# A head's half-tile products in one row, their operands partly in places of the mix, and the first decay differences held on VectorE

## The chip, the core and the metric

The kernel runs on one core of a Trainium2 chip. The core has four compute engines that run their own queues side by side: TensorE (PE, matmuls), VectorE (DVE), ScalarE (ACT) and GpSimd (POOL). SyncE (SP) issues most of the DMAs. The metric is the time on the device in microseconds (us); the median of the runs is compared.

## The reference

The program is a trunk of two decoder layers over 256 tokens of width 2048. Layer 0 mixes by chunked gated linear attention (GLA) with 4 heads (key width 256, value width 384), layer 1 by forgetting attention (FoX) with 12 heads. Both also attend to 256 memory tokens with 4 heads, and both end in a gated MLP with a short convolution. What matters here is the part of GLA inside a chunk, where each product of query and key carries a decay of its own:

```python
bcum = jnp.cumsum(gc, axis=2)
rel = bcum[:, :, :, None, :] - bcum[:, :, None, :, :]
decay = jnp.exp(jnp.where(tri, rel, -jnp.inf))
att = jnp.einsum('bhtk,bhsk,bhtsk->bhts', qc, kc, decay)
o_intra = jnp.einsum('bhts,bhsv->bhtv', att, vc)
```

and in FoX the difference of the summed log forget gates that is added to each logit:

```python
s = s + ci[..., None] - c[:, :, None, :]
```

## The kernel before

**Projections.** Nearly all the time goes into projections with float32 weights. A unit of weights comes in by DMA (line 198), ScalarE rounds it to float32r ("whi", L201), and VectorE makes the rest ("wlo", L210, the weight split). TensorE then makes three products of the rounded parts. `proj_fm` (L235, L236, L238) gives features by tokens, with 512 moving columns for whi (both parts of the activations) and 256 for wlo. `proj_tm` (L272, L273, L274) gives tokens by features. Whi and wlo have three buffers each, so a late split stops TensorE at the next L236 or L273.

**GLA.** For each head, `gates` makes the running sums of the log gates (L550 on TensorE, L553 to L555 on ScalarE, L557 to L559 on VectorE). Projections give q ("gq"), k ("gk") and v ("gv"); the v of head 0 is made ahead of everything else. Head 3 has two output gates ("og") between k and v. `core` then makes the 256x256 matrix `att` of a head:

- Products over chunk borders: q1 and k1 carry the decay to a border (L569 to L581); L585 is a 128x128 product, L589 are 4 half-tile products (a 128x64 weight tile, which goes to one half of the array and of PSUM's partitions), and L595 are 8 half-tile products of plain k and q for the diagonal.
- Inside chunks, three levels (blocks of 64, 16 and 4 tokens). For each level VectorE makes decay differences in `dd` (three L614), ScalarE their exponentials (L615), VectorE the product with q (three L617); for two of the levels k is scaled as well (L623 to L625, into `ks`). Then come 8 half-tile products (L631), and 6 predicated copies per level (L643) put the results into `att` by a mask.

`dd` has one buffer and the PSUM places of the tag "s" are two, used by each of these groups, by the gate matmuls (L550) and elsewhere. At the end L650 and L651 multiply `att` with v, and L659 applies the norm.

**FoX.** `attend` fetches a head's row of summed gates from DRAM (L749) and makes the differences `dm` on VectorE (L751, L753). It multiplies q and k (L755, L756), takes the softmax (L763, L765) and multiplies with v (L772, L773).

**Order.** The kernel is written in a tile framework. It gives every engine a fixed order of instructions from the order of the code, from priorities (weight loads and splits stand 300 steps ahead, `AHEAD`) and from its own estimate of when data is ready. On the chip each engine works through its queue in that order, and waits on semaphores. `tc.issue_after(i)` keeps an instruction behind another one in this order.

`bufA` and `bufB` are 16 tiles of 128 x 2 x 256 each. In GLA bufB holds the layer's input and bufA takes the result (`mix`), tile by tile: 12 to 15 from the memory attention, 0 to 11 from the output gates in `take_og`. Before that, bufA holds the memory tokens.

Of the kernel before, what the change touches and what calls it, by code (L numbers as in the profile page):

```python
# [19 lines left out]
P = 128  # L20
# [118 lines left out]
def _trunk(ctx: ExitStack, tc: tile.TileContext, xt, xtok, memt, wp, wgu, gns, gfin, cnv, par, msk, out):  # L139
# [28 lines left out]
    bufA = [const.tile([P, 2, T], F32R, name=f"A{i}") for i in range(KC)]  # L168
# [11 lines left out]
    loads, casts = [], []  # L180
# [67 lines left out]
    def proj_tm(key, src, evac, spare=None):  # L248

        units = where[key]
        n = units[0][2]
        base = min(min(u[1]) for u in units)
        acc = [pacc.tile([P, 512], F32, name="acc", tag="acc") for _ in range(2)]
        ahead = 0 if spare is None else 4
        ready = {}
        for i in range(len(units) + ahead):
            for b, u in ((0, i), (1, i - ahead)):
                if not 0 <= u < len(units):  # L260
                    continue
                if b == 0:
                    ready[u] = split_unit(units[u], pool=wpool if spare is None or u < 3 else spare)
                hi, lo = ready[u]
                kcs = units[u][1]
                a = acc[b][:, :n]
                xs = slice(b * P, (b + 1) * P)
                for j, kc in enumerate(kcs):
                    s = slice(j * n, (j + 1) * n)
                    xk = src[kc - base]  # L270
                    last = u == len(units) - 1 and j == len(kcs) - 1
                    TE.matmul(a, xk[:, 0, xs], hi[:, s], start=u == 0 and j == 0, stop=False)  # L272
                    TE.matmul(a, xk[:, 0, xs], lo[:, s], start=False, stop=False)  # L273
                    TE.matmul(a, xk[:, 1, xs], hi[:, s], start=False, stop=last)  # L274
                if u == len(units) - 1:
                    evac(b, a)
# [226 lines left out]
    def gla(nx):  # L503
        h, mix = bufB, bufA
        with tc.tile_pool(name="gla", bufs=1) as gp:
            att = [gp.tile([P, 3 * P], F32, name=f"att{i}") for i in range(2)]
            ks = [gp.tile([P, 2, T], F32, name=f"ks{i}") for i in range(2)]
# [54 lines left out]
            def core(hd, q, k, v, bc):  # L562
# [3 lines left out]
                q1 = gp.tile([P, 2, T], F32, name="gq1", tag="gq1")  # L566
                k1 = gp.tile([P, 2, T], F32, name="gk1", tag="gk1")
# [18 lines left out]
                for c in range(2):  # L586
                    for b in range(2):
                        lhs = k1[:, c, 128:192] if b else k1[:, c, 192:]
                        TE.matmul(ps[64 * b : 64 * (b + 1), P : P + 64], lhs, q1[:, c, P * b : P * b + 64],  # L589
                                  start=c == 0, stop=c == 1)  # L590
                for b in range(2):
                    for c in range(2):
                        for g in range(2):
                            gs = slice(b * P + 64 * g, b * P + 64 * (g + 1))
                            TE.matmul(ps[64 * g : 64 * (g + 1), T + b * 64 : T + (b + 1) * 64], k[:, c, gs], q[:, c, gs],  # L595
                                      start=c == 0, stop=c == 1)
                a3 = at.rearrange("p (b t) -> p b t", t=P)[:, 0:3:2, :]
# [3 lines left out]
                for g in range(2):  # L601
                    gs = slice(64 * g, 64 * (g + 1))
                    og = a3[gs, :, gs]
                    V.copy_predicated(og, ident[gs, gs].bitcast(I32).unsqueeze(1).to_broadcast(og.shape),
                                      ps[gs, T : T + P].rearrange("p (b t) -> p b t", t=64))
                for li, B in enumerate(LEVELS):
                    H = B // 4
                    ps = work("s", 2)
                    dd = gp.tile([P, 8, NVER], F32, name="gdd", tag="gdd")
                    b4, q4 = (t.rearrange("p d (g n t) -> p (d g) n t", g=4, t=B) for t in (bc, q))  # L610
                    parts = [(dd[:, :, o : o + w].rearrange("p a (n t) -> p a n t", t=(3 - i) * H), (i + 1) * H)
                             for i, (o, w) in enumerate(VERSIONS)]
                    for d, t0 in parts:
                        V.tensor_tensor(d, b4[:, :, :, t0:], b4[:, :, :, t0 - 1 : t0].to_broadcast(d.shape), ALU.subtract)  # L614
                    S.activation(dd, dd, AF.Exp, scale=1.0 / TAU)  # L615
                    for d, t0 in parts:
                        V.tensor_tensor(d, d, q4[:, :, :, t0:], ALU.mult)  # L617
                    if H > 1:
                        kt = ks[li % 2]
                        de = gp.tile([P, 2, T], F32, name="gde", tag="ed", bufs=2)  # L620
                        b5, k5, e5, kt5 = (t.rearrange("p d (n r t) -> p (d n) r t", r=4, t=H)[:, :, :3, :]
                                           for t in (bc, k, de, kt))
                        V.tensor_tensor(e5, b5[:, :, :, H - 1 :].to_broadcast(e5.shape), b5, ALU.subtract)  # L623
                        S.activation(e5, e5, AF.Exp, scale=1.0 / TAU)
                        V.tensor_tensor(kt5, k5, e5, ALU.mult)  # L625
                    else:
                        kt = k
                    for b in range(2):
                        for c in range(2):
                            for g in range(2):  # L630
                                TE.matmul(ps[64 * g : 64 * (g + 1), b * NVER : (b + 1) * NVER],  # L631
                                          kt[:, c, b * P + 64 * g : b * P + 64 * (g + 1)],
                                          dd[:, 4 * c + 2 * b + g, :], start=c == 0, stop=c == 1)
                    p3 = ps[:, : 2 * NVER].rearrange("p (b c) -> p b c", b=2)
# [52 lines left out]
            for j in range(OG_EARLY, 6):  # L687
                take_og(j)


    def fox(nx, vt):
        hk, hq, mix = bufB, bufA, bufB
        stash = vt.rearrange("p b (i t) -> p (b i) t", t=T)
        with (
# [39 lines left out]
            def take_mq(j):  # L734
                def evac(c, a):
                    q = fp.tile([P, T], F32, name="mq", tag="tmp", bufs=5)
                    V.scalar_tensor_tensor(q, whole(a), -(HD ** -0.5), nx.row(), ALU.mult, ALU.mult)
                    mem_attention(fp, 1, q, 2 * j + c, mix)

                proj_fm(("mq", 1, j), hq, evac)  # L740

            for j in range(2):
# [4 lines left out]
            def attend(hd, q):  # L747
# [3 lines left out]
                V.scalar_tensor_tensor(dm[:, :P], pb[:, :P], cc[:, 0, hd : hd + 1], foxmask[:, P:],  # L751
                                       ALU.subtract, ALU.add)
                V.scalar_tensor_tensor(dm[:, P:], pb[:, :T], cc[:, 1, hd : hd + 1], foxmask, ALU.subtract, ALU.add)  # L753
# [231 lines left out]
```

## Time and profile before

| | |
|---|---|
| median of 3 runs | 2298.16 us (2298.02 to 2298.43) |
| the profiled execution | 2298.03 us, span 2296.2 us |
| granted TensorE clock | 0.999 |
| TensorE busy | 2284.1 us (99%) |
| VectorE busy | 1619.1 us (71%) |
| ScalarE busy | 1253.6 us (55%) |
| HBM traffic | 186 GB/s over the span |

The span runs from the first to the last instruction of the profile. A row of the timeline has the start in us from the span's start, the time of the merged instructions in us, the engine, the line, the operation, the tiles it writes and reads, the shape and the number of instructions; in brackets stands the idle time before it and what ended that. The ends of matmuls are modelled and overlap, so start times tell what TensorE takes. A float32 matmul that is not float32r leaves two records. A row of a group has the number of instructions, then the busy time, the mean of one in ns, and the idle time before.

### The profile page before, as it was taken

The numbers are of one execution on the slowest core, as the hardware profiler recorded it, in microseconds if no ns is written. First come the engines' busy times: TensorE is split into PE (matmuls) and PEld (weight loads), VectorE is DVE, ScalarE is ACT, GpSimd is POOL, SyncE is SP. The second block draws the span as 40 slices with busy tenths as digits, with TensorE's granted clock in tenths as the row PEclk, the third lists the DMA queues.
The fourth block names the chain that finished last, engine by engine and source line by source line (L and its number), as shares of the span: only waits on it lengthen the run. The fifth ranks groups of instructions, "written<-read, shape, count | busy, mean of one in ns | idle before, by whom it ended". The sixth has DMA issues, their size and how long they took to land.

```text
span 2296.2 us, 33165 instructions
## 1 busy us (share of the span) xinstructions
PE 2284.1 (99%) x12384; PEld 1976.2 (86%) x12384; DVE 1619.1 (71%) x2667; ACT 1253.6 (55%) x1967; POOL 3.1 (0%) x20
## 2 busy tenths in 40 slices
PE   9999999999999999999999999999999999999998
PEld 7889888888888888888888998888888888888886
DVE  7578987577765777557767557657776577756775
ACT  7555555555553555445565455556554455534554
POOL 0000000000000000000000000000000000000000
PEclk9999999999999999999999999999999999999999
DMA  8655455555555555555555664555555555665554
GB/s 320 196 162 161 156 164 179 187 184 189 190 189 194 188 191 187 193 192 191 186 183 187 182 194 152 170 193 184 188 189 192 192 191 186 191 193 192 185 192 156
DMA packets 124745, 430.15 MB, mean 187 GB/s; under 512 B 14108, under 2 KB 18600, under 8 KB 124456
## 3 DMA queue, kind: packets, MB, share of 16 engines
q1 hardware_dynamic: 124152, 427.24, 57.3%
q8 instruction: 97, 1.59, 0.3%
q10 hardware_dynamic: 432, 0.79, 0.1%
q14 instruction: 64, 0.52, 0.1%
HBM read 425.87 MB, written 2.11 MB: 186 GB/s over the span
## 4 chain that ended last, share of the span: by engine, by line
PE 99%; DMA 0%; DVE 0%; ACT 0%; issue 0%; DVEq 0%; ACTq 0%; SPq 0%
PE acc L235 37%; PE acc L236 20%; PE acc L273 12%; PE acc L274 12%; PE acc L272 12%; PE acc L238 2%; PE ps_s L842 0%; PE ps_s L631 0%; PE ps_t L402 0%; PE ps_s L409 0%; PE ps_o L420 0%; PE ps_s L756 0%; PE ps_o L772 0%; PE ps_o L650 0%; DMA raw<-wp 0%; DMA cb<-cdram 0%
## 5 line engine op out<-in xcount | busy, mean ns | idle before, releaser
L210 DVE TENSOR_TENSOR wlo<-raw,whi 128x1024 fp32r<-128x1024 f32 (+4 forms) x812 | 972.8, 1199 | 542.3 <-ACT whi L201 531.3
L201 ACT ACTIVATE whi<-raw 128x1024 fp32r<-128x1024 f32 (+4 forms) x812 | 843.5, 1040 | 778.4 <-PE acc L274 373.7
L235 PE MATMUL acc<-B,whi 128*128 128x512 f32 x1980 | 683.6, 395 | 0.0
L235 PE MATMUL acc<-A,whi 128*128 128x512 f32 x1680 | 580.9, 397 | 1.3 <-DVE A L310 1.3
L236 PE MATMUL acc<-B,wlo 128*128 128x256 f32 x2112 | 550.0, 281 | 0.0
L236 PE MATMUL acc<-A,wlo 128*128 128x256 f32 x1792 | 464.0, 281 | 0.0
L235 PEld LDWEIGHTS acc<-B,whi 128*128 128x128 f32 x1980 | 360.7, 188 | 68.5
L236 PEld LDWEIGHTS acc<-B,wlo 128*128 128x128 f32 x2112 | 397.4, 188 | 21.9
L235 PEld LDWEIGHTS acc<-A,whi 128*128 128x128 f32 x1680 | 305.7, 188 | 58.7 <-DVE A L310 2.0
L236 PEld LDWEIGHTS acc<-A,wlo 128*128 128x128 f32 x1792 | 338.3, 189 | 20.2
L273 PE MATMUL acc<-wlo,B 128*128 128x512 f32 (+3 forms) x736 | 274.8, 374 | 0.9 <-DVE wlo L210 0.9
L274 PE MATMUL acc<-whi,B 128*128 128x512 f32 (+3 forms) x736 | 273.6, 372 | 0.0
L272 PE MATMUL acc<-whi,B 128*128 128x512 f32 (+3 forms) x736 | 247.2, 372 | 0.0
L273 PE MATMUL acc<-wlo,A 128*128 128x512 f32 x544 | 212.3, 390 | 0.0
L274 PE MATMUL acc<-whi,A 128*128 128x512 f32 x544 | 211.8, 389 | 0.0
L272 PE MATMUL acc<-whi,A 128*128 128x512 f32 x544 | 192.4, 390 | 0.0
L243 ACT ACTIVATE part<-acc 128x256 f32<-128x256 f32 x240 | 89.9, 375 | 156.7 <-PE acc L238 156.6
L273 PEld LDWEIGHTS acc<-wlo,B 128*128 128x128 f32 x736 | 138.2, 188 | 20.5 <-DVE wlo L210 1.2
L274 PEld LDWEIGHTS acc<-whi,B 128*128 128x128 f32 x736 | 138.2, 188 | 18.6
L272 PEld LDWEIGHTS acc<-whi,B 128*128 128x128 f32 x736 | 137.3, 188 | 18.7
L245 DVE TENSOR_TENSOR wholes<-acc,part 128x256 f32<-128x256 f32 x240 | 101.2, 422 | 64.2 <-ACT part L243 63.9
L274 PEld LDWEIGHTS acc<-whi,A 128*128 128x128 f32 x544 | 102.2, 188 | 21.1
(213 smaller groups left out, 1578.5 us busy)
## 6 DMA issues: line engine op xcount, KB each, us to landing
raw<-wp SPq DMA_DIRECT2D x743, 512.0 KB, 3.4
raw<-wp SPq DMA_DIRECT2D x32, 384.0 KB, 3.1
raw<-wp SPq DMA_DIRECT2D x24, 388.0 KB, 3.1
raw<-wp SPq DMA_DIRECT2D x8, 400.0 KB, 3.1
xf<-xt SPq DMA_DIRECT2D x16, 128.0 KB, 4.4
x<-xtok SPq DMA_DIRECT2D x4, 512.0 KB, 7.5
mt<-memt SPq DMA_DIRECT2D x3, 512.0 KB, 6.8
cb<-cdram SPq DMA_DIRECT2D x12, 128.0 KB, 3.2
```

What stands on the lines that cost most here:

```text
L201: casts.append(S.activation(hi[:, s], raw[:, s], AF.Copy))
L210: V.tensor_tensor(lo[:, s], raw[:, s], hi[:, s].bitcast(F32), ALU.subtract)
L235: TE.matmul(a, hi[:, s], both, start=done == 0, stop=False)
L236: TE.matmul(a[:, :T], lo[:, s], both[:, 0, :], start=False, stop=False)
L238: TE.matmul(a, hi[:, s], both, start=False, stop=True)
L243: S.activation(t, a[:, T:], AF.Copy)
L245: V.tensor_tensor(r, a[:, :T], t, ALU.add)
L272: TE.matmul(a, xk[:, 0, xs], hi[:, s], start=u == 0 and j == 0, stop=False)
L273: TE.matmul(a, xk[:, 0, xs], lo[:, s], start=False, stop=False)
L274: TE.matmul(a, xk[:, 1, xs], hi[:, s], start=False, stop=last)
```

## The change

- The three levels' operands are all made first. `dd` gets three buffers, one for each level. The products with q are held behind the last scaling of k (`issue_after(last.ins)`).
- Then all half-tile products of a head come in one row: 24 of the levels (levels 2, 1, 0), 4 of the chunk borders, 8 of the diagonal. Both "s" places hold the results. The 128x128 product L585 comes ahead, held behind the end of the last `proj_tm`; the row is held behind it, and the rest of the row behind the row's first product.
- The predicated copies follow for all levels together.
- `ks` (two tiles), q1 and k1 no longer have places of their own. They take those of the mix tiles 8 to 11 (of bufA) until output gates 4 and 5 need them.
- In FoX the differences `dm` are held on VectorE behind the scaling of the last memory query.

```diff
-    bufA = [const.tile([P, 2, T], F32R, name=f"A{i}") for i in range(KC)]
+    bufA = [const.tile([P, 2, T], F32R, name=f"A{i}", tag=f"A{i}") for i in range(KC)]
...
-                    TE.matmul(a, xk[:, 1, xs], hi[:, s], start=False, stop=last)
+                    mm = TE.matmul(a, xk[:, 1, xs], hi[:, s], start=False, stop=last)
+                    if last:
+                        ends.append(mm)
...
-            ks = [gp.tile([P, 2, T], F32, name=f"ks{i}") for i in range(2)]
+            place = iter(range(8, 12))
+            def lent(name):
+                return const.tile([P, 2, T], F32, name=name, tag=f"A{next(place)}")
+            ks = [lent(f"ks{i}") for i in range(2)]
+            gq1, gk1 = lent("gq1"), lent("gk1")
...
+                made = []
+                for li, B in enumerate(LEVELS):
+                    H = B // 4
+                    dd = gp.tile([P, 8, NVER], F32, name="gdd", tag="gdd", bufs=len(LEVELS))
...
+                    for d, t0 in parts:
+                        V.tensor_tensor(d, b4[:, :, :, t0:], b4[:, :, :, t0 - 1 : t0].to_broadcast(d.shape), ALU.subtract)
+                    S.activation(dd, dd, AF.Exp, scale=1.0 / TAU)
+                    if H > 1:
...
+                        last = V.tensor_tensor(kt5, k5, e5, ALU.mult)
+                    else:
+                        kt = k
+                    with tc.issue_after(last.ins):
+                        for d, t0 in parts:
+                            V.tensor_tensor(d, d, q4[:, :, :, t0:], ALU.mult)
+                    made.append((kt, dd))
+                ps, pl = work("s", 2), work("s", 2)
+                levels = (pl[:, : 2 * NVER], pl[:, 2 * NVER : 4 * NVER], ps[:, 512 - 2 * NVER :])
                 for c in range(2):
                     mov = q1[:, c, :].rearrange("p (n t) -> p n t", t=64)[:, 1:4:2, :]
-                    TE.matmul(ps[:, :P], k1[:, c, :P], mov, start=c == 0, stop=c == 1)
+                    with tc.issue_after(ends[-1].ins):
+                        first = TE.matmul(ps[:, :P], k1[:, c, :P], mov, start=c == 0, stop=c == 1)
+                for li in (2, 1, 0):
+                    kt, dd = made[li]
+                    for b in range(2):
+                        for c in range(2):
+                            for g in range(2):
+                                with tc.issue_after(first.ins):
+                                    mm = TE.matmul(levels[li][64 * g : 64 * (g + 1), b * NVER : (b + 1) * NVER],
+                                                   kt[:, c, b * P + 64 * g : b * P + 64 * (g + 1)],
+                                                   dd[:, 4 * c + 2 * b + g, :], start=c == 0, stop=c == 1)
+                                if (li, b, c, g) == (2, 0, 0, 0):
+                                    first = mm
+                with tc.issue_after(first.ins):
...
                 for li, B in enumerate(LEVELS):
                     H = B // 4
-                    ps = work("s", 2)
-                    dd = gp.tile([P, 8, NVER], F32, name="gdd", tag="gdd")
...
-                    p3 = ps[:, : 2 * NVER].rearrange("p (b c) -> p b c", b=2)
+                    p3 = levels[li].rearrange("p (b c) -> p b c", b=2)
...
             for j in range(OG_EARLY, 6):
+                for i in range(max(2 * j, 8), 2 * j + 2):
+                    mix[i] = const.tile([P, 2, T], F32R, name=f"mix{i}", tag=f"A{i}")
                 take_og(j)
...
-                    V.scalar_tensor_tensor(q, whole(a), -(HD ** -0.5), nx.row(), ALU.mult, ALU.mult)
+                    held.append(V.scalar_tensor_tensor(q, whole(a), -(HD ** -0.5), nx.row(), ALU.mult, ALU.mult))
...
+                with tc.issue_after(held[-1].ins):
+                    V.scalar_tensor_tensor(dm[:, :P], pb[:, :P], cc[:, 0, hd : hd + 1], foxmask[:, P:],
+                                           ALU.subtract, ALU.add)
+                    V.scalar_tensor_tensor(dm[:, P:], pb[:, :T], cc[:, 1, hd : hd + 1], foxmask,
+                                           ALU.subtract, ALU.add)
```

More of the change, by code (lines that the diff above doesn't have):

```diff
@@ L592, in core @@
+                with tc.issue_after(first.ins):
                     for c in range(2):
[L593 to L595 removed]
+                        for b in range(2):
+                            lhs = k1[:, c, 128:192] if b else k1[:, c, 192:]
+                            TE.matmul(ps[64 * b : 64 * (b + 1), P : P + 64], lhs, q1[:, c, P * b : P * b + 64],
@@ L596, in core @@
                                       start=c == 0, stop=c == 1)
+                    for b in range(2):
+                        for c in range(2):
+                            for g in range(2):
+                                gs = slice(b * P + 64 * g, b * P + 64 * (g + 1))
+                                TE.matmul(ps[64 * g : 64 * (g + 1), 192 + b * 64 : 192 + (b + 1) * 64],
+                                          k[:, c, gs], q[:, c, gs], start=c == 0, stop=c == 1)
                 a3 = at.rearrange("p (b t) -> p b t", t=P)[:, 0:3:2, :]
@@ L611, in core @@
[L611 to L627, printed above, removed]
```

33 lines of the change are left out of this document (13 added, 20 removed).

## The prediction

> **What bounds the kernel now.** I read the page first, then the waits of TensorE, then the timeline at single places. From the page:
>
> ```profile
> PE 2284.1 (99%) x12384; PEld 1976.2 (86%) x12384; DVE 1619.1 (71%) x2667; ACT 1253.6 (55%) x1967; POOL 3.1 (0%) x20
> ...
> PE 99%; DMA 0%; DVE 0%; ACT 0%; issue 0%; DVEq 0%; ACTq 0%; SPq 0%
> ```
>
> TensorE (PE) is busy from end to end, and the chain that ended last is TensorE alone. So the change can move the time in two ways only: by what the matmuls take from start to start, and by waits that appear on or vanish from TensorE. Work on VectorE (DVE), ScalarE or the queues counts only where TensorE waits for it. After the first microseconds the waits of TensorE hold one entry, in the later attention stage:
>
> ```profile
> PE acc L273 <- DVE wlo L210: 0.9, 1, 0.9
> ```
>
> **The change part by part. First, the visits to half-tile products.** A half-tile product (128x64 weights, lines 589, 595, 631) stands between full 128x128 matmuls. I read what one such visit takes from start times, since the modelled durations overlap:
>
> ```profile
> 190.29 0.28 PE L236 MATMUL acc<-B,wlo 128*128 128x256 f32 x1
> 190.50 0.88 PE L631 MATMUL ps_s<-gdd,ks 128*64 128x96 f32 x16
> 191.31 0.50 PE L235 MATMUL acc<-B,whi 128*128 128x512 f32 x1
> 191.65 0.28 PE L236 MATMUL acc<-B,wlo 128*128 128x256 f32 x1
> 191.77 0.40 PE L235 MATMUL acc<-B,whi 128*128 128x512 f32 x1
> 192.00 0.28 PE L236 MATMUL acc<-B,wlo 128*128 128x256 f32 x1
> ```
> ```profile
> 318.89 0.51 PE L272 MATMUL acc<-whi,B 128*128 128x384 f32 x2
> 319.34 0.33 PE L589 MATMUL ps_s<-gq,gk 128*64 128x64 f32 x2
> 319.60 0.45 PE L273 MATMUL acc<-wlo,B 128*128 128x384 f32 x1
> 319.88 0.34 PE L274 MATMUL acc<-whi,B 128*128 128x384 f32 x1
> 320.06 0.33 PE L272 MATMUL acc<-whi,B 128*128 128x384 f32 x1
> ...
> 321.10 0.33 PE L273 MATMUL acc<-wlo,B 128*128 128x384 f32 x1
> ```
> ```profile
> 329.66 0.34 PE L595 MATMUL ps_s<-gq,gk 128*64 128x64 f32 x4
> ```
>
> A product in plain float32 leaves two records, so the first visit holds a level's 8 products, the second a single one and the third two. First visit: from L236 at 190.29 to L236 at 191.65 are 1.36 us; a plain L236 and L235 take 0.35 us (0.12 and 0.23, 191.65 to 192.00); the visit costs 1.01 us. Second: from 318.89 to 320.06 are 1.17 us with four plain 384-column matmuls in it, at 0.174 us each (six of them from 320.06 to 321.10), 0.70 us; the visit costs 0.47 us. The third, read the same way, also costs 0.47 us: the two products go to the two halves of the array and run side by side. Let F be what a visit costs besides its products, and let a pair's time go with its columns: F + p = 0.47 for a pair of 64 columns and F + 4 x 1.5 p = 1.01 for four pairs of 96, so p = 0.11 and F = 0.36 us. F is the price of going to half tiles and back.
>
> How many visits? Each head has 4 + 8 + 24 products. Before, they come in the groups that the timeline shows between the first visit and the last:
>
> ```profile
> 179.90 0.45 PE L589 MATMUL ps_s<-gq,gk 128*64 128x64 f32 x8
> ...
> 351.95 0.88 PE L631 MATMUL ps_s<-gdd,gk 128*64 128x96 f32 x16
> ```
>
> I count 20: 3 in head 0, 4 each in heads 1 and 2 (a norm's matmul stands inside a group), and 9 in head 3, whose L589 and L595 come in ones, twos and fours. In the changed kernel's order there are 4: in every head the 36 products follow each other with nothing between. 16 visits less, at 0.36 us, are 5.8 us. Four single products of head 3 took a pair's time alone, and get partners: 2 x 0.11 more. **Sum: 6.0 us less.** Bounds: 5.3 (F at 0.33 by the roundings, and no partners) to 6.4 (also some 0.07 us per head for today's changes between 64 and 96 columns). Moving the L585 products ahead of the row costs nothing: they are 128x128.
>
> **Second, the differences held on VectorE.** The one wait above has its cause here:
>
> ```profile
> 1309.96 0.35 DVE L751 SCALAR_TENSOR_TENSOR dm<-cb,fcc,mask 128x128 f32<-128x128 f32 x1 [2.79 <-DMA cb<-cdram]
> ```
> ```profile
> 1310.23 0.51 PE L272 MATMUL acc<-whi,B 128*128 128x388 f32 x2
> 1311.64 0.44 PE L273 MATMUL acc<-wlo,B 128*128 128x388 f32 x1 [0.90 <-DVE wlo L210]
> ```
>
> VectorE stood 2.79 us in front of the first head's difference until a DMA had landed, and a weight split (L210) queued behind it. TensorE's start gap is 1.41 us for two matmuls of 0.18: 1.05 us lost. In the changed order all L751 and L753 come after the last memory query's scaling, two whole projections later and long after this DMA; the splits no longer stand behind them. What comes late next there? Nothing that I see: the first use of a difference is the attention of that same late stage. **1.05 us less** (0.90 by the wait's own row, the other bound).
>
> **Third, the price: VectorE's order in the linear attention.** Before, a level's decay differences (three L614) were made, used and evacuated before the next level's, since there was one buffer. Now there are three buffers, and in the changed order all nine differences of the next head stand ahead of the weight splits of the running value projection ("gv", L272 to L274), as soon as its gates are ready; and the 20 predicated copies of a head come in one batch after its row. So a split may come too late for TensorE. Rows for the sum:
>
> ```profile
> 208.25 0.56 DVE L614 TENSOR_TENSOR gdd<-bc 128x384 f32<-128x384 f32 x1
> 208.73 0.95 DVE L210 TENSOR_TENSOR wlo<-raw,whi 128x768 fp32r<-128x768 f32 x1
> 209.60 0.55 DVE L574 TENSOR_TENSOR gd<-bc 128x384 f32<-128x384 f32 x1
> 210.07 0.62 DVE L614 TENSOR_TENSOR gdd<-bc 128x256 f32<-128x256 f32 x2
> 210.60 0.55 DVE L571 TENSOR_TENSOR gq<-gq,ge 128x384 f32<-128x384 f32 x1
> 211.07 1.22 DVE L210 TENSOR_TENSOR wlo<-raw,whi 128x1024 fp32r<-128x1024 f32 x1
> ```
> ```profile
> 220.35 0.63 DVE L604 COPY_PREDICATED att<-mask,ps_s 64x128 f32<-64x128 int32 x2
> 221.01 1.10 DVE L614 TENSOR_TENSOR gdd<-bc 128x384 f32<-128x384 f32 x3
> ```
> ```profile
> L643 DVE COPY_PREDICATED att<-mask,ps_s 64x64 f32<-64x64 int32 x24 | 6.0, 251 | 0.7
> ```
> ```profile
> 249.93 0.48 DVE L557 TENSOR_SCALAR gm<-ps_s,part 128x256 f32<-128x256 f32 x1
> ...
> 251.95 0.93 DVE L210 TENSOR_TENSOR wlo<-raw,whi 128x768 fp32r<-128x768 f32 x1
> ```
> ```profile
> 210.56 0.59 PE L650 MATMUL ps_o<-att,gv 128*128 128x256 f32 x2
> 210.99 0.39 PE L651 MATMUL ps_o<-att,gv 128*128 128x128 f32 x2
> 211.13 0.42 PE L272 MATMUL acc<-whi,B 128*128 128x384 f32 x1
> 211.39 0.34 PE L273 MATMUL acc<-wlo,B 128*128 128x384 f32 x1
> ```
>
> From start to start a level's differences take 0.48 + 0.53 = 1.01 us, a 768-column split 0.87, L574 and L571 0.47 each, two L604 0.66 (0.33 each). A plain 128x256 step takes about 0.34 (the x2 row: 0.53 for one of 256 and one of 128). For the copies of L643 I take the middle form's 0.25 and the gap of 0.03 that the L604 rows show. The gate steps (L557 to L559, with one L546) are 2.0 us from 249.93 to 251.95; the second half, without L546, is about 1.5.
>
> Head 1's value projection. I start both engines at the last product of head 0's row. TensorE, up to the L273 that needs the split behind the nine differences, has in the changed order 16 L236 (0.118), 14 L235 and L238 (0.233), 74 of the 384-column matmuls (0.174), two gate matmuls (0.12) and three L650 with L651 (210.56 to 211.39, less one plain: 0.65), and leaves the row (0.3): 1.9 + 3.3 + 12.9 + 0.2 + 2.0 + 0.3 = **20.6 us**. VectorE starts 0.9 later (an estimate: a matmul's drain and three short copies of ScalarE come first), and has no idle time after that: 2 L604 and 18 L643 (0.7 + 5.0), 5 splits (4.4), 4 steps that take k (1.4), the gates (3.5), nine differences (3.0), L574, L571 and one sum of squares (1.3), and then the split itself (0.95): 0.9 + 20.2 = **21.1 us**, or 21.3 with the small gaps between steps that depend on each other. TensorE waits 0.5 to 0.7 us; I take 0.7.
>
> Head 2 alike, from the row of head 1. TensorE up to its L273: 48 L236, 46 L235 and L238, 26 of 384 columns, three L650 with L651, four of 256 columns, and out of the row: 5.6 + 10.7 + 4.5 + 2.0 + 0.5 + 0.3 = 23.6. VectorE: 0.9, copies with a norm's short steps between them 5.8, two L368 0.7, three wide splits (211.07's 1.22 less 0.08 of overlap) 3.5, takes of q and k 1.8, gates 3.5, three L659 1.2 (as a plain step of 0.34 with a gap), two splits 1.75, nine differences 3.0, the other three steps 1.3, the split 0.95: 24.4, with those gaps 24.7. TensorE waits 0.8 to 1.1 us; I take 1.1, and 0.2 to 0.3 once more at the next split, ahead of which key differences and a product stand. Head 3 has two output gates' projections ahead of its values, and its gates are ready in wider-spaced work: no wait by the same sum. **Sum of new waits: 2.1 us.** Bounds: these are small differences of sums above 20 us, so 2% of VectorE's sums (0.4 us each, and the second carries on) decide much: 0.8 to 3.6 us.
>
> The Trainium skill, in TensorEngine Tiling (Array Packing), section PSUM Bottleneck, speaks against the change: tiling speeds up TensorE but not the emptying of PSUM, which may become what limits. By that rule alone the batch of 20 copies would take back the gain that the row brings; by the rows above the copies are no more than before and only move, so the sum goes by the rows (rival B is the rule's case).
>
> **What else moves, at nothing.** The four lent places (two key buffers, q1, k1) are the mix's tiles 8 to 11. On POOL the clearing of the key buffers now waits for the last memory projection to have read them, and the clearing of "narrow" is queued behind it; its user stands at the end of the first value projection, one whole projection later. On the other side the output gates 4 and 5 must wait for head 3's row, which is done two projections before them. The row holds both "s" banks, so the next head's gate matmuls wait for all 20 copies; in the changed order they stand 80 and more matmuls behind the row, some 6.7 us, about what the copies and the start need; it is the closest of these, and is covered by the same bounds. The row itself waits for all of a head's operands; by sums of the same kind they are ready 1.4 to 3 us ahead of it (an estimate). If that cover went, the wait would be one for one. ScalarE changes its function table less often in the changed order; it is not on the chain.
>
> **Sum.** The profiled execution took 2298.03 us (span 2296.2), 0.13 under the median of 2298.16. 2298.03 - 6.0 - 1.05 + 2.1 = **2293.1**; 0.13 is far inside the bounds, so this stands for the median too.
>
> **The rivals.** A, no new waits (under 0.8 us): VectorE's splits come in time, as they do in the whole trace of before. For it: in the profile there is but the one wait. Against: the nine differences alone are 2.0 us more ahead of a split than today's three. 2298.0 - 7.0 = 2291.0, up to 2291.8.
>
> B, emptying becomes the limit: copies and differences push the splits of heads 1, 2 and 3 back by some 1.2 us more in all, and the gate matmuls wait for the "s" banks. Waits 3.0 to 5.0 us: 2294.0 to 2296.0. For it: VectorE has no idle time noted in any of the rows shown from 208 to 221 us. Against it: the copies are few and short, and the sums above have them in. (This is the case that the Trainium skill's section PSUM Bottleneck speaks of.)
>
> C, slower: the row stands too early in TensorE's order and waits for its operands. In a head before, the products of level 0 came first and the other two levels were made while TensorE went on. If the row stood at the old first place, TensorE would wait for two levels: differences 1.0, products with q 1.0 and a key scaling 0.9, some 5 us per head, 20 in all: 2298.0 - 7.0 + 20 = 2311. It decides from 7 us of waiting in all, 1.8 per head. Against it: in the order of the changed kernel VectorE's last operand stands ahead of the row with 1.4 us and more to spare.
>
> D, the change doesn't do what it says: F isn't the price of the visit but of these products, and goes along into the row. Then only the wait of 1.05 us goes and the 2.1 come: 2299. Against it: two products cost what one costs.
>
> **How the numbers follow.** Forecast (waits of 0.8 to 3.0 us: 2291.8 to 2294.0) 0.60, A 0.10, B 0.24, C 0.03, D 0.03. 0.2% of the time is 4.6 us, about what a measurement can tell from no change: below 2293.6 is faster. That takes A and nine tenths of the forecast: 0.10 + 0.54 = 0.64. Slower than 2302.8 is C alone, 0.03. The rest, 0.33, is the same. The range leaves out the low half of A, the top of B, C and D: 2291.2 to 2295.4.
>
> **What would show it.** Right: four blocks of 72 half-tile records in TensorE's timeline, each some 2.9 us; no L273 waiting near 1311 us; new entries of L273 waiting for a split (L210) in the value projections of heads 1 and 2, together some 2 us. Wrong: a half-tile record that waits for VectorE's products (C), gate matmuls that wait for copies (B), blocks of 4 us and more (D).

## The result and the profile after

The changed kernel takes **2293.43 us** (median of 15 runs, lowest 2293.01) against 2298.1 for the kernel before, a ratio of 0.998 with a 95% interval of 0.9973 to 0.9986. The forecast was 2293.1 in a range of 2291.2 to 2295.4. One of the 15 runs took 3232.78 us at a granted clock of 0.654, and the ratio leaves it out. The profiled execution took 2293.43 us with a span of 2291.3, so the span is 4.9 us shorter, and 0.3 us more lies outside it (2.1 against 1.8).

The page of the changed kernel, its engines and its chain:

```profile
PE 2277.9 (99%) x12384; PEld 1973.3 (86%) x12384; DVE 1616.7 (71%) x2667; ACT 1250.3 (55%) x1965; POOL 3.2 (0%) x20
...
PE 98%; DVE 2%; issue 0%; DMA 0%; ACT 0%; DVEq 0%
```

The same 12384 matmuls are busy for 6.2 us less, and VectorE (DVE) now has 2% of the chain that ended last, where it had 0%. The waits of TensorE in the changed kernel say where (total, times, longest):

```profile
PE ps_o L178 <- DVE B L175: 1.4, 1, 1.4
PE acc L235 <- DVE A L312: 1.4, 1, 1.4
PE acc L273 <- DVE wlo L210: 1.4, 2, 0.7
PE acc L236 <- DVE wlo L210: 0.6, 1, 0.6
```

The first two were there before. The wait of 0.9 us in FoX is gone; two waits for a weight split (L210) in value projections of the linear attention have come, 1.4 us together. The 0.6 us of L236 stand at 19.81 us, in the start-up, where the changed kernel was 0.87 us ahead until then and is within 0.1 us of the other afterwards: it cancels, and I leave it out.

The new row of head 0, from TensorE's timeline of the changed kernel (the chunk products are now L627, the border ones L636, the diagonal ones L642):

```profile
186.19 0.63 PE L235 MATMUL acc<-B,whi 128*128 128x512 f32 x2
186.75 0.88 PE L627 MATMUL ps_s<-gdd,gk 128*64 128x96 f32 x16
187.46 1.49 PE L627 MATMUL ps_s<-gdd,ks 128*64 128x96 f32 x32
188.78 0.40 PE L636 MATMUL ps_s<-gq,gk 128*64 128x64 f32 x8
189.01 0.64 PE L642 MATMUL ps_s<-gq,gk 128*64 128x64 f32 x16
189.58 0.50 PE L236 MATMUL acc<-B,wlo 128*128 128x256 f32 x2
189.92 0.39 PE L235 MATMUL acc<-B,whi 128*128 128x512 f32 x1
```

All 72 half-tile records follow each other. From L235 at 186.19 to L235 at 189.92 are 3.73 us; the two L235 and two L236 in it would take 0.70, so the row costs 3.03 us. The four heads cost 3.02, 3.03, 3.03 and 3.04 us, 12.1 in all, where the 20 visits before, read in the same way, cost 17.6 to 18.1, depending on what is put down to the 128x128 products that stand in or next to them (L585, L334): **5.5 to 6.0 us less**.

The two new waits, in TensorE's timeline of the changed kernel (heads 1 and 2):

```profile
209.57 0.51 PE L272 MATMUL acc<-whi,B 128*128 128x384 f32 x2
210.76 0.44 PE L273 MATMUL acc<-wlo,B 128*128 128x384 f32 x1 [0.68 <-DVE wlo L210]
...
248.82 0.44 PE L273 MATMUL acc<-wlo,B 128*128 128x384 f32 x1 [0.67 <-DVE wlo L210]
```

Two L272 take 0.35 us from start to start; here 1.19 pass, so the first wait costs 0.84 us, and the second as much by the same reading: 1.68 us. The L273 behind each wait then takes 0.28 us to the next start (L274 at 211.04 and at 249.10) where a plain one takes 0.174, so the two places cost 0.95 and 0.94 us.

A third split was late, the next one in head 2. The list of waits lacks it, because the modelled ends of the matmuls cover the gap; the start times have it, in TensorE's timeline and below it VectorE's:

```profile
250.69 0.51 PE L272 MATMUL acc<-whi,B 128*128 128x384 f32 x2
251.16 0.44 PE L273 MATMUL acc<-wlo,B 128*128 128x384 f32 x1
251.44 0.34 PE L274 MATMUL acc<-whi,B 128*128 128x384 f32 x1
```

```profile
250.14 0.96 DVE L210 TENSOR_TENSOR wlo<-raw,whi 128x768 fp32r<-128x768 f32 x1
```

The split ends at 251.10, and from 250.69 to 251.44 are 0.75 us for three matmuls of 0.174: 0.23 us lost. Late splits cost **2.12 us** in all.

What VectorE did ahead of the first of them, in its timeline of the changed kernel:

```profile
190.34 0.63 DVE L651 COPY_PREDICATED att<-mask,ps_s 64x128 f32<-64x128 int32 x2 [2.23 <-ACT att L647]
191.00 3.74 DVE L664 COPY_PREDICATED att<-mask,ps_s 64x96 f32<-64x96 int32 x14
...
205.36 0.56 DVE L599 TENSOR_TENSOR gdd<-bc 128x384 f32<-128x384 f32 x1
205.83 0.55 DVE L582 TENSOR_TENSOR gd<-bc 128x384 f32<-128x384 f32 x1
206.30 2.74 DVE L599 TENSOR_TENSOR gdd<-bc 128x256 f32<-128x256 f32 x8
...
209.75 0.95 DVE L210 TENSOR_TENSOR wlo<-raw,whi 128x768 fp32r<-128x768 f32 x1
```

The copies of head 0 begin at 190.34, and the split that TensorE needs at 210.76 starts at 209.75, behind nine differences (L599). And in FoX, at the place of the former wait, TensorE's timeline of the changed kernel:

```profile
1310.47 0.51 PE L272 MATMUL acc<-whi,B 128*128 128x388 f32 x2
1310.82 0.34 PE L273 MATMUL acc<-wlo,B 128*128 128x388 f32 x1
```

L273 follows in 0.35 us. Before, L272 at 1310.23 to L274 at 1311.92 were 1.69 us for three matmuls of 0.177, so this place cost 1.16. In the changed kernel another split came late a little further on: from L272 at 1312.58 to L274 at 1313.32 are 0.74 us for the same three, 0.21 lost. Ahead of that split ScalarE had waited 2.87 us until a weight DMA landed (its L201 at 1311.13).

Counted between the same projection matmuls of both kernels, the linear attention (177.6 to 394.7 us before) takes 213.11 us instead of 217.05, 3.94 less; the stretch around that wait in FoX (1183 to 1595 us before) takes 0.95 us less, which is 1.16 less 0.21. Together 4.89 of the span's 4.9.

### The profile page after: what moved, and what is told of

It reads as the page before. It is cut to its first block, busy times and chain, and to the rows that moved or that the text cites. A ratio compares the mean times of both kernels' runs of the same rounds, so it can differ in the third digit from the quotient of the medians.

```text
span 2291.3 us, 33157 instructions
## 1 busy us (share of the span) xinstructions
PE 2277.9 (99%) x12384; PEld 1973.3 (86%) x12384; DVE 1616.7 (71%) x2667; ACT 1250.3 (55%) x1965; POOL 3.2 (0%) x20
## 4 chain that ended last, share of the span: by engine, by line
PE 98%; DVE 2%; issue 0%; DMA 0%; ACT 0%; DVEq 0%
PE acc L235 37%; PE acc L236 20%; PE acc L273 12%; PE acc L274 12%; PE acc L272 12%; PE acc L238 2%; DVE wlo L210 0%; PE ps_s L869 0%; PE ps_s L627 0%; PE ps_t L404 0%; PE ps_s L411 0%; PE ps_o L422 0%; DVE gdd L599 0%; PE ps_s L783 0%; PE ps_o L799 0%
## 5 line engine op out<-in xcount | busy, mean ns | idle before, releaser
L210 DVE TENSOR_TENSOR wlo<-raw,whi 128x1024 fp32r<-128x1024 f32 (+4 forms) x812 | 972.3, 1199 | 546.8 <-ACT whi L201 535.6
L201 ACT ACTIVATE whi<-raw 128x1024 fp32r<-128x1024 f32 (+4 forms) x812 | 843.4, 1040 | 774.9 <-PE acc L274 367.2
L235 PE MATMUL acc<-B,whi 128*128 128x512 f32 x1980 | 682.4, 395 | 0.0
L236 PE MATMUL acc<-B,wlo 128*128 128x256 f32 x2112 | 548.5, 280 | 0.0
L235 PE MATMUL acc<-A,whi 128*128 128x512 f32 x1264 | 438.5, 396 | 1.5 <-DVE A L312 1.4
L235 PEld LDWEIGHTS acc<-B,whi 128*128 128x128 f32 x1980 | 360.3, 188 | 67.8
L236 PEld LDWEIGHTS acc<-B,wlo 128*128 128x128 f32 x2112 | 397.4, 188 | 22.0 <-DVE wlo L210 0.2
L236 PE MATMUL acc<-A,wlo 128*128 128x256 f32 x1376 | 353.4, 280 | 0.7 <-DVE wlo L210 0.6
L273 PE MATMUL acc<-wlo,B 128*128 128x512 f32 (+3 forms) x736 | 274.6, 373 | 1.4 <-DVE wlo L210 1.4
L236 PEld LDWEIGHTS acc<-A,wlo 128*128 128x128 f32 x1376 | 258.6, 188 | 17.7 <-DVE wlo L210 1.5
L274 PE MATMUL acc<-whi,B 128*128 128x512 f32 (+3 forms) x736 | 273.6, 372 | 0.0
L235 PEld LDWEIGHTS acc<-A,whi 128*128 128x128 f32 x1264 | 230.0, 188 | 43.8 <-DVE A L312 2.0
L272 PE MATMUL acc<-whi,B 128*128 128x512 f32 (+3 forms) x736 | 246.6, 371 | 0.0
L273 PE MATMUL acc<-wlo,A 128*128 128x512 f32 x416 | 162.5, 391 | 0.0
L274 PE MATMUL acc<-whi,A 128*128 128x512 f32 x416 | 161.9, 389 | 0.0
L273 PEld LDWEIGHTS acc<-wlo,B 128*128 128x128 f32 x736 | 138.2, 188 | 21.5 <-DVE wlo L210 2.5
L274 PEld LDWEIGHTS acc<-whi,B 128*128 128x128 f32 x736 | 138.3, 188 | 18.8
L272 PEld LDWEIGHTS acc<-whi,B 128*128 128x128 f32 x736 | 137.4, 188 | 18.6
L272 PE MATMUL acc<-whi,A 128*128 128x512 f32 x416 | 147.8, 391 | 0.0
L235 PE MATMUL acc<-mix,whi 128*128 128x512 f32 x416 | 146.4, 398 | 0.0
```

Source lines behind the costliest of these rows:

```text
L201: casts.append(S.activation(hi[:, s], raw[:, s], AF.Copy))
L210: V.tensor_tensor(lo[:, s], raw[:, s], hi[:, s].bitcast(F32), ALU.subtract)
L235: TE.matmul(a, hi[:, s], both, start=done == 0, stop=False)
L236: TE.matmul(a[:, :T], lo[:, s], both[:, 0, :], start=False, stop=False)
L274: mm = TE.matmul(a, xk[:, 1, xs], hi[:, s], start=False, stop=last)
```

## The experiments

My theory: a round trip from the whole array to half tiles and back costs F = 0.36 us beside the products, and nothing else of TensorE's work changed; the differences on VectorE make the new waits. The rivals: the row pays for something else (the places, the buffers, the pairing); the emptying of PSUM makes the waits.

**held_alone**: the kernel before, with the FoX part of the change only.

```diff
+                    held.append(V.scalar_tensor_tensor(q, whole(a), -(HD ** -0.5), nx.row(), ALU.mult, ALU.mult))
...
+                with tc.issue_after(held[-1].ins):
                     V.scalar_tensor_tensor(dm[:, :P], pb[:, :P], cc[:, 0, hd : hd + 1], foxmask[:, P:],
```

> The kernel before with the FoX differences held behind the last memory query's scaling, and nothing else of the change. My theory (the wait of TensorE at 1311 us came from a weight split queued behind a difference that waited for its DMA): that wait goes, nothing else moves, 1.05 us less than before, 2297.1 us; TensorE has no wait on VectorE after the first microseconds. Rival (the wait moves: the splits are late for the forget gates' chain anyway): a wait of some 1 us stays near there and the time stays at 2298.1 us.

Measured: 2297.31 us against 2298.41 on the same chip. The ratio of 0.9995 has an interval of 0.9986 to 1.0004, which holds no change, so the stretches decide. The waits of TensorE in this kernel:

```profile
PE acc L235 <- DVE A L310: 1.9, 1, 1.9
PE ps_o L178 <- DVE B L175: 1.4, 1, 1.4
```

The L273 entry is gone, and nothing has taken its place (the start-up wait of L235, 1.3 us before, is 0.6 us longer in this execution). The FoX stretch is 1.18 us shorter, the linear attention unchanged at 217.05. Held differences are worth the wait that they blocked, about 1.1 us.

**row_broken_full** and **row_broken_half**: the changed kernel, with one product of 16 columns put in between the levels of each row, two per head. In the first it uses the whole array, so that each row is left and entered again twice; in the control it uses a half tile and the row stays whole.

```diff
+                    if li < 2:
+                        w = P if 1 else 64      # 64 in row_broken_half
+                        with tc.issue_after(mm.ins):
+                            first = TE.matmul(pl[:w, 384:400], ones[:, :w], ident[:, :16], start=True, stop=True)
...
-                with tc.issue_after(first.ins):
+                with tc.issue_after(mm.ins):
```

> The changed kernel, with one extra product of 16 columns on the whole 128x128 array (result unused, plain float32) between the levels of each row: 8 in all, so the row is left and entered twice more per head. My theory (F is the price of going from half tiles to the whole array and back): each adds 0.36 us and about 0.03 for itself, 3.1 us in all in the rows, each row 3.8 instead of 3.0 us. Rival (F belongs to the change between float32r and plain float32, or to the products): no such change is added, so 0.03 to 0.1 us each, under 1 us in all.

> Control to the broken row: the same 8 extra products of 16 columns at the same places, but on a half tile (64 columns of weights), so that the row stays in half tiles. My theory: 0.03 to 0.1 us each, under 0.8 us in all, each row at most 3.2 us. Rival (any foreign product in the row, another weight load or another bank place costs the 0.36): like the broken row, 3.1 us.

Measured: 2298.45 and 2294.46 us (before: 2298.41). TensorE's timeline of row_broken_full, head 0 (the dummy is L626):

```profile
186.24 0.63 PE L235 MATMUL acc<-B,whi 128*128 128x512 f32 x2
186.80 0.88 PE L631 MATMUL ps_s<-gdd,gk 128*64 128x96 f32 x16
187.61 0.40 PE L626 MATMUL ps_s<-mask 128*128 128x16 f32 x2
187.94 0.88 PE L631 MATMUL ps_s<-gdd,ks 128*64 128x96 f32 x16
188.75 0.40 PE L626 MATMUL ps_s<-mask 128*128 128x16 f32 x2
...
190.92 0.40 PE L235 MATMUL acc<-B,whi 128*128 128x512 f32 x1
```

and of row_broken_half:

```profile
186.42 0.63 PE L235 MATMUL acc<-B,whi 128*128 128x512 f32 x2
186.98 0.88 PE L631 MATMUL ps_s<-gdd,gk 128*64 128x96 f32 x16
187.69 0.18 PE L626 MATMUL ps_s<-mask 128*64 128x16 f32 x1
...
190.38 0.39 PE L235 MATMUL acc<-B,whi 128*128 128x512 f32 x1
```

Read as above, the broken row costs 4.68 - 0.70 = 3.98 us and the control 3.96 - 0.70 = 3.26 (3.25 on the mean of four heads): (3.98 - 3.25) / 2 = **0.364 us** for one round trip, the products being the same in number and columns. That is F. (The control's row is 0.22 us above the changed kernel's 3.03, a little more than was expected.) Eight round trips are 2.9 of the 4.0 us between the medians. The rest is waiting: head 2's wait for its split, 0.79 us in the control, is 1.9 in the broken kernel.

**mlp_lone_half**, **mlp_lone_full**, **mlp_row_half**: F by itself, far from the linear attention. The changed kernel gets 44 useless products of 64 moving columns in the up-projections of the first MLP: one by one on a half tile, one by one on the whole array, or all 44 half-tile ones in a row.

```diff
+                        def more(mm):
+                            w = 64           # 128 in mlp_lone_full
+                            for i in range(1):   # 44, at one place, in mlp_row_half
+                                ...
+                                with tc.issue_after(mm.ins):
+                                    mm = TE.matmul(..., ones[:, :w], mask[:, M_FOX : M_FOX + 64], start=True, stop=True)
```

> The changed kernel with 44 extra half-tile products (64 columns of weights, 64 moving columns, plain float32, result unused), one in each up-projection of the first MLP, alone between float32r matmuls. My theory: 0.47 us each as in the linear attention before, 20.7 us in all, 2314.1 us. Rival (the price of 0.36 us belongs to the linear attention: its operands, its busy VectorE): 0.05 to 0.15 us each, 2296 to 2300 us.

> Control: the same 44 extra products at the same places, but with 128 columns of weights, so on the whole array; number format and moving columns are the same. My theory (the price is the half tile's, not the number format's): 0.11 us each, 4.7 us in all, 2298.1 us. Rival (going from float32r to plain float32 and back costs it): 0.47 us each, 2314.1 us.

> The same 44 extra half-tile products as one row in one up-projection, the two halves in turn. My theory: one F of 0.36 and 22 pairs of 0.107, 2.7 us, 2296.1 us. Rival (each product pays for itself): 20 us.

Measured spans, less the changed kernel's 2291.3: 23.0 us (0.52 each), 7.9 us (0.18 each) and 2.8 us. The lone products are 0.05 us (half tile) and 0.07 us (whole array) dearer than expected, and their difference, 0.34 each by the spans and 0.355 by the medians (2316.66, of two runs, and 2301.04), is F again. The 2.8 us of the row come from the fastest of its eight runs; by the medians on that chip (2297.09, and 2293.79 for the changed kernel) the row costs 3.3. Either is near the 2.7 expected and far from the rival's 20: in a row F is paid once. One visit in TensorE's timeline of mlp_lone_half:

```profile
489.69 0.28 PE L236 MATMUL acc<-B,wlo 128*128 128x256 f32 x1
489.89 0.33 PE L863 MATMUL ps_o<-mask 128*64 128x64 f32 x2
...
490.49 0.28 PE L236 MATMUL acc<-B,wlo 128*128 128x256 f32 x1
```

and the same of mlp_lone_full:

```profile
489.71 0.28 PE L236 MATMUL acc<-B,wlo 128*128 128x256 f32 x1
489.82 0.33 PE L863 MATMUL ps_o<-mask 128*128 128x64 f32 x2
...
490.27 0.28 PE L236 MATMUL acc<-B,wlo 128*128 128x256 f32 x1
```

From L236 to L236 the half tile takes 0.80 and the whole array 0.56 us, 0.24 apart. Behind a later visit the same 43 plain matmuls take 7.53 us in the one kernel (560.67 to 568.20) and 7.41 in the other (558.51 to 565.92). On the mean of the 44 visits the two kernels are 0.24 us apart at the second matmul behind the visit and 0.34 at the 44th. So about a third of F's price stands behind the visit and not in it. Why is open.

**differences_later**: the changed kernel with the differences of the second and third level held behind the key scaling of the level before, so that six of nine stand no longer ahead of the splits. (What the changed kernel itself holds on VectorE are the differences `dm` of FoX; the decay differences in `dd` are held in this experiment alone.)

```diff
-                    for d, t0 in parts:
-                        V.tensor_tensor(d, b4[:, :, :, t0:], b4[:, :, :, t0 - 1 : t0].to_broadcast(d.shape), ALU.subtract)
+                    with (tc.issue_after(last.ins) if li else nullcontext()):
+                        for d, t0 in parts:
+                            V.tensor_tensor(d, b4[:, :, :, t0:], b4[:, :, :, t0 - 1 : t0].to_broadcast(d.shape),
+                                            ALU.subtract)
```

> The changed kernel, with the decay differences of the second and third level held on VectorE behind the key scaling of the level before. The amount of work stays the same, only its place in VectorE's order moves. My theory (the two waits of 0.84 us for splits in heads 1 and 2 come from nine differences standing ahead of the split): those waits fall from 1.7 to some 0.3 us in the value projections, and up to 1.2 us come back later, at the first splits behind (L236), since VectorE has little slack in a head; 0.5 to 1.0 us less than the changed kernel, 2292.4 to 2292.9 us. Rival (the batch of 20 copies is what makes the splits late, whatever the differences do): the waits stay at the same splits with 1.5 us or more, and the time is the same or higher.

Measured: **2291.8 us** (before: 2298.41; ratio 0.9972, interval 0.9961 to 0.9983). VectorE's timeline of this kernel, head 1 (the differences are L600):

```profile
209.57 0.56 DVE L600 TENSOR_TENSOR gdd<-bc 128x384 f32<-128x384 f32 x1
...
210.86 0.62 DVE L600 TENSOR_TENSOR gdd<-bc 128x256 f32<-128x256 f32 x2
211.39 1.22 DVE L210 TENSOR_TENSOR wlo<-raw,whi 128x1024 fp32r<-128x1024 f32 x1
```

Three differences are left here, and the list of waits has no matmul of the value projections (by the starts one split of head 2 is still 0.15 us late, at 248.48). What came back later is one wait of 0.39 us (0.56 by the starts), in TensorE's timeline:

```profile
260.23 0.61 PE L622 MATMUL ps_s<-gq,gk 128*128 128x128 f32 x4
261.23 0.51 PE L236 MATMUL acc<-B,wlo 128*128 128x256 f32 x2 [0.39 <-DVE wlo L210]
```

The linear attention takes 211.66 us, 5.40 less than before; with the 0.56 that it still waits, 5.96, about the row's whole worth. I had expected 0.5 to 1.0 us from this and got 1.6: the waits were the differences' work, as the theory has it, but I thought that more of them would only move.

**copies_left_out**: the changed kernel without the copies of levels 2 and 3, 12 of a head's 20, so that `att` keeps old values there.

```diff
-                    for i, (o, w) in enumerate(VERSIONS):
+                    for i, (o, w) in enumerate(VERSIONS if li == 0 else ()):
```

> The changed kernel without the predicated copies of the second and third level (12 of 20 per head; att keeps old values there). It takes 3.3 us of VectorE's work per head out of the batch behind the row; the nine differences stay where they are. Rival (the batch of copies makes the splits late): the waits of 1.7 us in heads 1 and 2 go. My theory (a sum of queued work, in which the differences' place decides) expects the same sign here, since less work queued ahead of the split helps whatever it is: waits of 0 to 0.2 us, 2291.7 to 2292.0 us. So it does not tell the two apart by itself; it bounds what the copies can be blamed for: if more than 0.5 us of waits stays, they are not the cause at all.

Measured: 2291.41 us (before: 2298.33), no matmul of the linear attention in the list of waits, its stretch 211.50 us; a little below what was expected. Taking some 3 us of copies per head out of VectorE's queue frees the splits as well as taking six differences from ahead of them does. So the two experiments do not set copies against differences; they say that the splits were late by less than either. But differences_later keeps every copy: the emptying of PSUM was not the limit, the order was.

**buffers_alone** and **places_alone**: the kernel before with three `dd` buffers and the lent places, and with the lent places only; no row and no FoX part in either.

```diff
-            ks = [gp.tile([P, 2, T], F32, name=f"ks{i}") for i in range(2)]
+            ks = [lent(f"ks{i}") for i in range(2)]
+            gq1, gk1 = lent("gq1"), lent("gk1")
...
+                    dd = gp.tile([P, 8, NVER], F32, name="gdd", tag="gdd", bufs=3)   # buffers_alone only
```

> The kernel before with the four lent places and three buffers for the decay differences, but without the row, the holding in FoX and the holding of the products with q. My theory (what costs is VectorE's order: with three buffers the differences move ahead of splits): new waits of TensorE for splits in heads 0 to 2, 2 to 6 us in all, so 2300 to 2304 us, slower than before. Rival (the waits come with the row, because the copies come in one batch): no new waits, 2298.1 us.

> The kernel before with the four lent places (two key buffers, q1, k1 in the mix's tiles 8 to 11) and nothing else. My theory: nothing on TensorE's path waits for these places, 2298.1 us (2298.0 to 2298.4). Rival (clearing them on GpSimd behind the last memory projection, or the output gates 4 and 5 behind the last head, makes something late): 0.3 us or more above that, with a new wait in the value projection of head 0 or at the output gates.

Measured: 2305.49 us (ratio 1.0031, interval 1.002 to 1.0043) and 2298.53 (1.0001, 0.9991 to 1.0011), against 2298.33. The places cost nothing. The buffers without the row and without the hold on the products with q cost 7.2 us, more than I had thought. The largest entry among the waits of TensorE in buffers_alone:

```profile
PE acc L273 <- DVE wlo L210: 3.9, 3, 2.6
```

With free buffers the levels' products with q (L623 here) also move ahead of splits; in the changed kernel they are held (`issue_after(last.ins)`). The worst place, on VectorE and then on TensorE, from the two timelines of buffers_alone:

```profile
252.18 1.17 DVE L623 TENSOR_TENSOR gdd<-gdd,gq 128x384 f32<-128x384 f32 x3
253.28 0.94 DVE L210 TENSOR_TENSOR wlo<-raw,whi 128x768 fp32r<-128x768 f32 x1
```

```profile
254.28 0.69 PE L273 MATMUL acc<-wlo,B 128*128 128x384 f32 x1 [2.62 <-DVE wlo L210]
254.76 0.52 PE L274 MATMUL acc<-whi,B 128*128 128x384 f32 x1
255.09 0.52 PE L272 MATMUL acc<-whi,B 128*128 128x384 f32 x1
```

and its granted clock there (window, length, TensorE busy, clock, DMA share, GB/s):

```profile
254.20:257.30 3.10, 3.02 (x9) 0.50 0.67 158
257.30:260.40 3.10, 3.10 (x19) 1.00 0.75 255
```

After 2.62 us in which TensorE waited, the next matmuls of 384 columns start 0.32 to 0.33 us apart instead of 0.174, at a granted clock of 0.50, until 257.3 us. Nine of them take 3.04 us instead of 1.57: this wait cost some 1.5 us more than its length.

**changed_again** and **later_again**: both kernels once more, though not on one chip as was intended.

> The changed kernel once more, beside the version with the later differences on the same chip: 2293.4 us (2293.0 to 2294.0).

> The version with the differences of the second and third level held behind the key scaling of the level before, once more, as the best version so far. From its first run: 2291.8 us (2291.5 to 2292.6), 1.4 to 1.8 us less than the changed kernel; in the linear attention one wait of some 0.6 us in place of two of 0.84. If it was luck of one chip: 2293 us or more.

Measured: 2293.79 us (2293.14 to 2294.49; ratio 0.998, interval 0.9971 to 0.9989), before 2298.39 on the same chip, and 2292.05 (2291.61 to 2292.35; 0.9973, 0.9962 to 0.9983), before 2298.32 on another. The two chips are 0.07 us apart in the kernel before, and the slowest run of the second kernel is faster than the fastest of the first: the version with the differences held later is 1.7 us faster than the changed kernel, and 6.3 us faster than the kernel before.

## Why the prediction was right

**What bounds the kernel.** Held: 4.89 of the span's 4.9 us are start gaps of TensorE or waits on it. VectorE's share of busy time (71%) did not change and told nothing; the place of three splits in its order did.

**The visits, forecast -6.0: right**, -5.5 to -6.0 by the rows, -5.96 by differences_later, and -6.06 by the changed kernel's linear attention (-3.94 less the 2.12 of the late splits). F was forecast as 0.36 and measured as 0.364 in the row and 0.34 to 0.355 in the MLP. The rows cost 3.02 to 3.04 us instead of some 2.9, 0.5 in all; the difference held because the visits before cost up to 18.1 us by the same reading, and not the 17.6 that 6.0 and four rows of 2.9 imply. The Trainium skill, in TensorEngine Tiling (Array Packing), section Key Properties, says that a change of tiling mode drains the array first, without a price; the broken row fits that with a price of 0.364 us, though no run here shows that a drain is what costs it. Rival D (the price belongs to the products and goes along) is excluded by the pair of broken rows.

**The FoX wait, forecast -1.05: right**, -1.16 by the starts, -1.18 in the stretch of held_alone. The changed kernel gained 0.95, because another split came 0.21 us late behind a weight DMA. "Nothing that I see" for what comes late next was therefore not quite so in that execution, but held_alone has no such loss.

**The new waits, forecast 2.1: right in place, cause and sum, 2.12.** All three places came as forecast: head 1 (0.7 forecast, 0.95 measured), head 2 (1.1 and 0.94), and the split that follows in head 2 (0.2 to 0.3 and 0.23), ahead of which stand a key difference (L606) and a product (L700). That the sum agrees to 0.02 is partly luck, since the first two errors partly cancel. In head 1 VectorE's side was 21.3 us from the row's last product to the end of the split, as forecast, and TensorE's 20.5 instead of 20.6; the rest of the 0.95 is the slower L273 behind the wait, which the sum did not have. In head 2 TensorE's side was 23.5 instead of 23.6, and VectorE's 24.3: the rows had added up to 24.4, and the 0.3 that was put on top for gaps between dependent steps was not there. Rival A (no new waits) is out, but differences_later shows it to be one hold away.

**Rival B** (emptying becomes the limit) did not occur. There is no gate matmul that waits for copies, and the waits went with the same copies in the queue. The Trainium skill, in TensorEngine Tiling (Array Packing), section PSUM Bottleneck, says that the copies out of PSUM may become the limit once tiling has sped TensorE up fourfold. Here, with two half tiles, they were not the limit, and counted only as part of VectorE's queue ahead of a split.

**Rival C** (the row waits for its operands) did not occur: no half-tile record waits. But its price of one for one was too mild: buffers_alone shows a stop of 2.62 us that cost 1.5 us more, at half the clock.

**The lent places**, put at nothing, cost nothing: places_alone is 0.2 us from the kernel before, within the interval.

**The sum.** -6.0 + 2.12 in the linear attention is -3.9, measured -3.94; -1.16 + 0.21 in FoX is -0.95; and 0.3 us more lie outside the span.

## What to carry to other kernels

When a kernel is bound by one engine from end to end, price a reordering by that engine's start gaps, visit by visit, and then look for the waits that the new order makes elsewhere, by the starts as well as in the list of waits, which lacked one of three here: here 16 round trips at 0.36 us were worth 6 us, and 1.7 us of the result hung on where six subtractions stand in VectorE's queue. Buffers let a scheduler move ready work ahead of urgent work, so look at what moves when you add one: here the same buffers cost 7.2 us without the row and the hold. Which of the two was missed, no run tells apart. A start gap of 0.84 us cost 0.95 with the matmul behind it; the stop of 2.62 us also halved the clock for the next 3 us.

## What the runs showed of the hardware

- **A stop can lower the clock** (seen at one stop). In buffers_alone the granted clock went to 0.50 with a wait of 2.62 us and stayed there until 3 us of matmuls had passed; in row_broken_full a wait of 1.74 us (252.13 us) left it at 1.00. The Trainium skill, TensorE: Matmul & The Clock Gate, Part 1, has the half clock after an idle window of about 3.4 us, free-running; here less idle time was enough.
- **F does not hang on the number format.** It is 0.364 us between two groups of plain float32 products and 0.34 to 0.355 between float32r and float32.
- **VectorE overlaps successive instructions, but not where the start partition changes.** In the timeline of the changed kernel above, L582 starts at 205.83, 0.09 us before the 0.56 us of L599 from 205.36 are over. The 14 copies from 191.00 switch between the halves of the partitions and take 0.27 us each from start to start (3.77 us to the next instruction at 194.77), without that overlap. It is not the copy itself: in head 2 the copy to the lower half at 225.37 (0.30 us) is overlapped by 0.09 us by a step on all partitions (L346, at 225.57, 0.15 us), and the copy to the upper half starts 0.03 us after that step, at 225.75.
